# The two norms at the edge between mixer and feed-forward: fewer weight sums on TensorE, the head's steps in another order, and the last range written out by two queues

## The chip, the cores and the metric

The kernel runs on one core of a Trainium2 chip. The metric is the device time of one execution in microseconds (us). Before the change its median over three runs is 1840.19 us (1839.05 to 1841.2). About 0.2% of that, 3.7 us, is what a measurement of this kernel can tell from no change.

## What is computed

The reference is a two-layer encoder in fp32 that runs over a prompt of 256 positions and a sample of 512, both with 1024 channels. Layer 0 mixes positions with a bidirectional mLSTM, layer 1 with sliding-window attention. Behind each mixer stands a feed-forward block with a convolution of width 3 (2816 hidden channels), and at the end one more norm:

```
for l in range(2):
    h = rmsnorm(x, norm_g[l,0]) * (1+sc1) + sh1
    x = x + g1 * mixer_l(h)                        # ends with ... @ w_out
    h = rmsnorm(x, norm_g[l,1]) * (1+sc2) + sh2
    x = x + g2 * conv_ffn(h)                       # h @ w_up, conv, silu(g)*val, @ w_down
y = rmsnorm(x, final_g)
rmsnorm(x, g) = x * rsqrt(mean(x*x) + EPS) * g
```

The change touches the way in which the norm in front of each feed-forward block is made, the first steps of that block, and the last norm's output.

## The kernel before

**Layout.** Both sequences stand side by side in 768 columns; the 1024 channels are 8 chunks c of 128 partitions. Work on the columns goes in two HALVES of 384, or, at the end of the kernel, in RANGES of 256. A matrix product is made as three single-pass products of high and low parts (hi times hi, lo times hi, hi times lo). The high part of a tile is a ScalarE copy (L260) and the low part a VectorE subtraction (L261). TensorE (PE) issues in its program's order, and so does every other engine.

**The norm (class Norm, L90 to L165).** `square(c)` squares one chunk on ScalarE (L111 of the profile), and VectorE adds squares into one sum tile (L115) for as long as fewer than KC minus `on_pe` have come, so that `on_pe` squares stay apart. `stages()` sums over partitions with PE: for each of the three blocks of 128 columns one two-column matmul per remaining tile ("weight sums", `pa<-inv,nt`, 128x2). With `on_pe` = 2 three tiles remain, so nine matmuls, which the profile shows as 18 records. ScalarE then makes `nr` (L150), GpSimd (POOL) raises it to the power -1/2 (L153, "pow"), and three matmuls spread it over all partitions (`pa<-kct,nr`, "spread", six records). `apply` scales the half by the result.

**out_proj (L592 to L630)** makes 16 products of 128 channels: 0 to 7 for the first half, 8 to 15 for the second. Each is 24 matmuls into one of four PSUM banks in turn; behind it VectorE adds it to x (the residual, L590), and ScalarE squares the new chunk. The norm's remaining steps for the first half run between the second half's products (`tick`), with `combined`'s `apply` (L1095): 16 scalings L1090, a ScalarE bias, and a split into yh and yl. For the second half `apply` makes a longer chain (L1113, L1130, L1126 and so on), which begins with `dsh` (L1108), a subtraction of 4 numbers per partition.

**head (L1257 to L1369)** is the feed-forward block's start. It runs for PE, ScalarE and VectorE in the order in which it is written (`manual_schedule`). It takes `last_tile`, the rest of out_proj, which yields ahead of product 15. So what is in head ahead of `for _ in last_tile` (L1300) stands between product 14 and product 15 on PE: the two `mark` matmuls (`ps<-yh`, values that nothing reads) into banks 2 and 3, which held products 12 and 13. On VectorE stand there `sums(0)` (L1282 to L1287, sums of weights). Then come product 15, and `outset` (L1184), that is 12 products on the quarter B11 (the first half's chunks 0 to 3), a ScalarE copy of that bank (L1189), and 12 products on B21 into the same bank. Between B11 and B21 `step()` (L1306) puts the second half's nine weight sums, behind B21 its spread, and a second `outset` follows. `pair` (L1194) makes the following parts; its sums of weights are POOL's (L1202, L1205, L1206, L1214).

**The end.** The last RANGE's norm takes the spread factor `pr` in one PSUM bank. ScalarE copies it to SBUF (L574, `side`). POOL multiplies chunks 2, 5 and 7 by `side` (L579), VectorE the other five by `pr` (L581), and the sync engine (SP) issues the eight stores, in the order of c (L582).

## Time and profile before

| what | us |
|---|---|
| median of the three runs | 1840.19 |
| the profiled execution's own time | 1839.38 |
| its span, first to last instruction | 1837.3 |
| PE busy | 1792.4 (98%) |
| VectorE busy | 1373.0 (75%) |
| ScalarE busy | 893.9 (49%) |
| POOL busy | 486.6 (26%) |

Times within the execution are counted from the span's start. In rows of the timeline the first number is the start, the second the duration, and a bracket holds the idle time of the engine just before with what ended it. Rows of matmuls overlap, since one begins before the end of the other: the distance of starts is what one costs. Layer 0's head lies about 500 to 520, layer 1's about 1285 to 1305, and the end from 1828 on. The granted TensorE clock is 0.993 in the mean; in the last 12 us it is 0.50 to 0.63.

### The profile page before, as it was taken

How to read it: one execution, taken by the hardware profiler on the slowest of the kernel's cores; microseconds unless marked ns; L12 is line 12 of the kernel's file. 1: busy time of each engine (PE TensorE's matmuls, PEld its weight loads, DVE VectorE, ACT ScalarE, POOL GpSimd, SP SyncE). 2: the span in 40 equal slices, each digit the busy share in tenths (PEclk: the TensorE clock that was granted, in tenths of full speed). 3: DMA queues.
4: the chain of work that ended last, by engine and by line, in shares of the span. 5: the costliest groups of instructions: out<-in, count | busy, mean ns of one | idle time of the engine just before them, and what ended most of it. 6: DMA issues, size and time to landing. Idle time of an engine off the chain costs nothing.

```text
span 1837.3 us, 28927 instructions
## 1 busy us (share of the span) xinstructions
PE 1792.4 (98%) x11290; PEld 1657.9 (90%) x11290; DVE 1373.0 (75%) x2101; ACT 893.9 (49%) x1815; POOL 486.6 (26%) x386
## 2 busy tenths in 40 slices
PE   6999999999999999999999999999999999999997
PEld 3987887889998999999999999889889999999997
DVE  4755676886689877777777867766898777787876
ACT  4444443344456444444444557665464444444443
POOL 1001001031024333333331313320234333333322
PEclk9999999999999999999999999999999999999998
DMA  8344556546312212222222331234122222222212
GB/s 332 118 147 134 172 195 223 164 140 213 104 46 71 79 58 69 69 70 69 69 69 83 114 92 42 61 97 127 46 81 70 69 69 70 70 69 70 69 35 69
DMA packets 64245, 184.48 MB, mean 100 GB/s; under 512 B 6167, under 2 KB 23831, under 8 KB 64108
## 3 DMA queue, kind: packets, MB, share of 16 engines
q1 hardware_dynamic: 64108, 182.63, 30.7%
q8 instruction: 89, 1.46, 0.3%
q14 instruction: 48, 0.39, 0.1%
HBM read 176.17 MB, written 6.43 MB: 99 GB/s over the span
## 4 chain that ended last, share of the span: by engine, by line
PE 87%; DVE 5%; DMA 3%; ACT 2%; issue 1%; POOL 1%; SPq 0%; POOLq 0%; ACTq 0%; DVEq 0%
PE ps L254 29%; PE pa L254 24%; PE ps L1169 10%; PE ps L1172 10%; PE ps L1170 10%; PE pa L1008 1%; DMA slab<-in_adaln_w_dram 1%; DMA raw<-in_adaln_w_dram 1%; DMA raw<-in_w_dram 1%; DVE wlo L261 1%; DVE ada L506 1%; PE pa L1169 0%; PE pa L1172 0%; PE pa L1170 0%; DMA slab<-mrows 0%
## 5 line engine op out<-in xcount | busy, mean ns | idle before, releaser
L260 ACT CAST whi<-raw 128x1024 fp32r<-128x1024 f32 x237 | 247.9, 1048 | 344.2 <-PE pa L254 145.6
L261 DVE TENSOR_TENSOR wlo<-raw,whi 128x1024 fp32r<-128x1024 f32 x237 | 321.7, 1358 | 112.9 <-ACT whi L260 110.5
L254 PE MATMUL pa<-slab,whi 128*128 128x256 f32 (+1 forms) x1328 | 317.2, 334 | 0.0
L254 PEld LDWEIGHTS pa<-slab,whi 128*128 128x128 f32 x1328 | 230.2, 189 | 21.8 <-DVE slab L590 0.2
L590 DVE SCALAR_TENSOR_TENSOR slab<-pa,mod,slab 128x256 f32<-128x256 f32 (+1 forms) x332 | 192.8, 598 | 65.1 <-PE pa L254 65.0
L254 PE MATMUL pa<-slab,wlo 128*128 128x256 f32 (+1 forms) x664 | 212.7, 333 | 0.0
L254 PE MATMUL ps<-zh,whi 128*128 128x256 f32 (+1 forms) x560 | 189.2, 339 | 2.2 <-ACT whi L260 1.6
L254 PE MATMUL ps<-zh,wlo 128*128 128x256 f32 (+1 forms) x560 | 183.9, 330 | 1.7 <-DVE wlo L261 1.7
L254 PE MATMUL ps<-zl,whi 128*128 128x256 f32 (+1 forms) x560 | 185.0, 333 | 0.5 <-DVE zl L552 0.5
L1169 PE MATMUL ps<-zh,whi 128*128 128x384 f32 x504 | 172.2, 342 | 3.7 <-ACT nt L1240 1.9
L1170 PE MATMUL ps<-zl,whi 128*128 128x384 f32 x504 | 169.9, 337 | 1.8 <-DVE zl L1126 1.8
L1172 PE MATMUL ps<-zh,wlo 128*128 128x384 f32 x504 | 168.9, 335 | 0.0
L254 PE MATMUL ps<-slab,whi 128*128 128x384 f32 (+2 forms) x656 | 163.1, 332 | 0.9 <-DVE slab L261 0.5
L1205 POOL TENSOR_TENSOR raw<-raw,raw 128x512 f32<-128x512 f32 x40 | 52.0, 1299 | 331.0 <-DVE wlo L261 246.4
L254 PEld LDWEIGHTS pa<-slab,wlo 128*128 128x128 f32 x664 | 125.2, 189 | 12.6 <-DVE wlo L261 0.4
L1402 POOL TENSOR_TENSOR slab<-slab 128x772 f32<-128x772 f32 x44 | 86.5, 1968 | 166.0 <-DVE slab L1390 154.0
L1389 DVE SCALAR_TENSOR_TENSOR slab<-slab,cstt,slab 128x771 f32<-128x771 f32 x88 | 104.6, 1190 | 26.7 <-ACT slab L1387 26.5
L254 PEld LDWEIGHTS ps<-zh,whi 128*128 128x128 f32 x560 | 107.4, 192 | 15.8 <-issue 4.4
L506 DVE SCALAR_TENSOR_TENSOR ada<-raw,silc,ada 128x1024 f32<-128x1024 f32 x84 | 110.2, 1350 | 14.7 <-DMA raw<-in_adaln_w_dram 14.7
L254 PEld LDWEIGHTS ps<-zl,whi 128*128 128x128 f32 x560 | 107.4, 193 | 12.7 <-issue 3.4
L1202 POOL TENSOR_TENSOR raw<-raw 128x512 f32<-128x512 f32 x40 | 65.6, 1639 | 201.0 <-DMA raw<-in_w_dram 167.8
L254 PEld LDWEIGHTS ps<-slab,whi 128*128 128x128 f32 x656 | 115.1, 188 | 3.4 <-ACT whi L260 0.9
(291 smaller groups left out, 4336.7 us busy)
## 6 DMA issues: line engine op xcount, KB each, us to landing
raw<-in_w_dram SPq DMA_DIRECT2D x208, 512.0 KB, 3.7
raw<-in_adaln_w_dram SPq DMA_DIRECT2D x84, 512.0 KB, 4.6
slab<-in_x_dram SPq DMA_DIRECT2D x12, 512.0 KB, 7.9
slab<-in_adaln_w_dram SPq DMA_DIRECT2D x12, 512.0 KB, 10.2
slab<-mrows SPq DMA_DIRECT2D x8, 384.0 KB, 5.6
xs<-slab SPq DMA_DIRECT2D x6, 512.0 KB, 3.2
bt<-brow SPq DMA_DIRECT2D x16, 192.0 KB, 3.1
slab<-xs SPq DMA_DIRECT2D x6, 512.0 KB, 5.8
```

The source lines that it names most:

```text
L254: self.nc.tensor.matmul(out, lhsT, rhs, start=start, stop=stop)
L260: nc.scalar.copy(hi, src)
L261: return nc.vector.tensor_tensor(lo, src, hi.bitcast(F32), ALU.subtract)
L506: stt(acc[:, s], row, w, acc[:, s], ALU.mult, ALU.add)
L590: self.nc.vector.scalar_tensor_tensor(x, o, self.mod[l][:, gc + c, q : q + 1], x, ALU.mult, ALU.add)
L1169: mm(o, wh[:, k], hi[k], start=start and k == 0, stop=False, skip_group_check=True)
L1170: mm(o, wh[:, k], lo[k], start=False, stop=False, skip_group_check=True)
L1172: mm(o, wl[:, k], hi[k], start=False, stop=k == 3, skip_group_check=True)
L1202: tt(q[2], q[2], q[3], ALU.add)
L1205: tt(q[0], q[2], q[0], ALU.subtract)
L1389: stt(y[:, 1:], u[:, :-1], w(0), y[:, 1:], ALU.mult, ALU.add)
L1402: nc.gpsimd.tensor_tensor(y, y, yrow[:, j], ALU.mult)
```

## The change

1. `Norm` takes `on_pe` = 0 for the first half and 1 for the second: VectorE adds all eight squares, or seven, and three or six weight-sum matmuls remain. `held` keeps the add of the last two products out of `square`, so that head can place it; `begin` may put the first three of the second half's six ahead of B11.
2. `out_proj` yields ahead of product 14, and around the residuals of the last two products, and head uses that to place `sums(0)`, `sums(1)`, the splits, residuals and squares in an order of its own.
3. The `marks` therefore stand ahead of product 14 rather than ahead of 15.
4. The first `outset`'s quarters put their eight products with high weights first, then a step of the second half's norm (`low=step`), then the four with low weights.
5. `dsh` is made by the first half's `apply`.
6. POOL's pow is handed on as a third instruction to `behind`, so that `pair` for the first following part has its POOL work issued behind the second half's pow.
7. At the end the last range's factor is spread into two banks (`twin`); ScalarE copies the second, VectorE reads the first. Chunk 7 goes from POOL to VectorE; chunks 1, 2, 5 and 7 are stored by ScalarE's queue.

PE, the last two products in layer 0 (ps_4535 and ps_4536 are the banks of products 12 and 13, ps_4533 and ps_4534 those of 14 and 15). Before:

```order
L254 MATMUL ps_4533<-slab_3919,whi_5099 128x384 x2
L254 MATMUL ps_4533<-slab_3919,wlo_5100 128x384
L254 MATMUL ps_4535<-yh 128x384
L254 MATMUL ps_4536<-yh 128x384
L254 MATMUL ps_4534<-slab_3916,whi_5132 128x384 x2
L254 MATMUL ps_4534<-slab_3916,wlo_5133 128x384
```

and now:

```order
L266 MATMUL ps_4536<-slab_3919,whi_5063 128x384 x2
L266 MATMUL ps_4536<-slab_3919,wlo_5064 128x384
L266 MATMUL ps_4535<-yh 128x384
L266 MATMUL ps_4536<-yh 128x384
L266 MATMUL ps_4533<-slab_3916,whi_5097 128x384 x2
L266 MATMUL ps_4533<-slab_3916,wlo_5098 128x384
```

The marks have moved from behind product 14 to behind product 13, and the second mark now overwrites the bank that the matmul right ahead of it has just filled.

VectorE, around the residual of product 15 (ps_4534) and up to the second half's chain, before:

```order
L261 TENSOR_TENSOR wlo_5170<-raw_5145,whi_5169 128x1024
L590 TENSOR_SCALAR slab_4542<-ps_4534,mod_88,slab_4542 128x384
L1282 TENSOR_TENSOR raw_5151<-raw_5151 128x512
L1284 TENSOR_TENSOR raw_5149<-raw_5151,raw_5149 128x512
L1285 TENSOR_TENSOR raw_5149<-raw_5149 128x512
L1286 TENSOR_TENSOR slab_5142<-raw_5151,slab_5142 128x512
L1287 TENSOR_TENSOR raw_5151<-raw_5151,raw_5149 128x512
L261 TENSOR_TENSOR wlo_5233<-raw_5149,whi_5232 128x1024
L1108 TENSOR_TENSOR dsh<-mod_88 128x4
L1113 TENSOR_SCALAR slab_5254<-slab_4542,gain_91,pa_5250 128x384
```

and now:

```order
L1322 TENSOR_TENSOR wlo_5139<-raw_5116,whi_5138 128x1024
L120 TENSOR_TENSOR nt_4874<-nt_4874,nt_5166 128x384
L1308 TENSOR_TENSOR raw_5122<-raw_5122 128x512
L1310 TENSOR_TENSOR raw_5120<-raw_5122,raw_5120 128x512
L605 TENSOR_SCALAR slab_4542<-ps_4534,mod_88,slab_4542 128x384
L1312 TENSOR_TENSOR raw_5120<-raw_5120 128x512
L1314 TENSOR_TENSOR slab_5113<-raw_5122,slab_5113 128x512
L1315 TENSOR_TENSOR raw_5122<-raw_5122,raw_5120 128x512
L1322 TENSOR_TENSOR wlo_5208<-raw_5120,whi_5207 128x1024
L1139 TENSOR_SCALAR slab_5244<-slab_4542,gain_91,pa_5240 128x384
```

An add of squares (L120) and two of the sums have come ahead of the last residual, and the chain follows the last split at once, without `dsh`.

POOL at the same place, before (nr_5223 is the second half's factor; the raw tiles are weights of the following part):

```order
L153 TENSOR_TENSOR nr_4873<-nr_4873,mhalf 128x3
L1202 TENSOR_TENSOR raw_5579<-raw_5579 128x512
L1380 MEMSET slab_5136 128x4x4
L1380 MEMSET slab_5137 128x4x4
L1205 TENSOR_TENSOR raw_5581<-raw_5579,raw_5581 128x512
L153 TENSOR_TENSOR nr_5223<-nr_5223,mhalf 128x3
L1206 TENSOR_TENSOR raw_5581<-raw_5581 128x512
```

and now:

```order
L160 TENSOR_TENSOR nr_4870<-nr_4870,mhalf 128x3
L1420 MEMSET slab_5107 128x4x4
L1420 MEMSET slab_5108 128x4x4
L160 TENSOR_TENSOR nr_5224<-nr_5224,mhalf 128x3
L1228 TENSOR_TENSOR raw_5573<-raw_5573 128x512
L1231 TENSOR_TENSOR raw_5575<-raw_5573,raw_5575 128x512
L1232 TENSOR_TENSOR raw_5575<-raw_5575 128x512
```

The second half's power now stands ahead of the two sums of weights that it stood behind.

The diff, without its last hunk, which only hands `self.norm.power.ins` on as a third value of head:

```diff
@@ -110,10 +110,16 @@
         sq = net.tmp([P, self.n])
         net.nc.scalar.activation(sq, self.x(c), AF.Square)
         self.sums.append(sq)
-        if 2 <= len(self.sums) and self.count < KC - self.on_pe:
+        self.count += 1
+        if not self.held:
+            self.add()
+
+    def add(self):
+        if 2 <= len(self.sums) and self.count <= KC - self.on_pe:
             acc = self.sums[0]
             self.adds.tensor_tensor(acc, acc, self.sums.pop(), ALU.add)
-        self.count += 1
+
+    held = False
 
     count = 0
 
@@ -123,12 +129,13 @@
             self.pm = self.net.pa()
             self.sides = [self.pm[:, 2 * b : 2 * b + 2] for b in range(self.n // P)]
             self.done = 0
-        for i in range(self.done, n):
+        last = min(KC, self.on_pe + 1) - 1
+        for i in range(self.done, min(n, last + 1)):
             for b, o in enumerate(self.sides):
 
                 self.net.nc.tensor.matmul(
                     o, self.sums[i][:, b * P : (b + 1) * P], self.net.inv,
-                    start=i == b == 0, stop=i == KC - 1, skip_group_check=True,
+                    start=i == b == 0, stop=i == last, skip_group_check=True,
                 )
         self.done = max(self.done, n)
 
@@ -150,12 +157,17 @@
             nc.scalar.activation(r, mean, AF.Copy, bias=EPS)
         else:
             nc.vector.tensor_scalar(r, mean, EPS, None, ALU.add)
-        nc.gpsimd.tensor_tensor(r, r, net.mhalf[:, :nb], ALU.pow)
+        self.power = nc.gpsimd.tensor_tensor(r, r, net.mhalf[:, :nb], ALU.pow)
         yield 2.0
 
-        pr = net.pa()[:, : self.n]
-        for b in range(nb):
-            net.mm(pr[:, b * P : (b + 1) * P], r[:, b : b + 1].to_broadcast([P, P]), net.ident, True, True)
+        def spread():
+            pr = net.pa()[:, : self.n]
+            for b in range(nb):
+                net.mm(pr[:, b * P : (b + 1) * P], r[:, b : b + 1].to_broadcast([P, P]), net.ident, True, True)
+            return pr
+
+        pr = spread()
+        net.twin = spread() if self.on_pe == KC and self.last else None
         yield from self.apply(self.x, pr, self.rng)
 
     def run(self):
@@ -571,15 +583,18 @@
     def output(self, x, pr, rng):
         nc = self.nc
         side = self.tmp([P, rng[1] - rng[0]])
-        nc.scalar.copy(side, pr)
+        end = rng is RANGES[-1]
+        nc.scalar.copy(side, self.twin if end else pr)
         for c in range(KC):
 
-            if c in ((2, 5, 7), (0, 2))[rng is RANGES[1]]:
+            turn = c in ((2, 5, 7), (0, 2), (2, 5))[2 if end else rng is RANGES[1]]
+            if turn:
                 nc.scalar.activation(x(c), x(c), AF.Copy, scale=self.cst(FG + c))
                 nc.gpsimd.tensor_tensor(x(c), x(c), side, ALU.mult)
             else:
                 nc.vector.scalar_tensor_tensor(x(c), x(c), self.cst(FG + c), pr, ALU.mult, ALU.mult)
-            self.nc.sync.dma_start(self.io["y"][:, c, rng[0] : rng[1]], x(c))
+            queue = nc.scalar if end and c in (1, 2, 5, 7) else nc.sync
+            queue.dma_start(self.io["y"][:, c, rng[0] : rng[1]], x(c))
             if c % 2:
                 yield 1.3
 
@@ -606,7 +621,8 @@
                 for h, w in self.halves(u0 + u):
                     yield 1, 2 * u + h, w
 
-        norms = [Norm(self, xt, half, apply, last=True, adds=self.nc.vector) for half in HALVES]
+        norms = [Norm(self, xt, half, apply, i, last=True, adds=self.nc.vector) for i, half in enumerate(HALVES)]
+        self.norm = norms[1]
 
         self.turn = 1
         todo = tiles()
@@ -616,16 +632,26 @@
             for i, (z, c, w) in enumerate(first):
                 self.product(self.bank[2 + i][:, :H], w, act, 0, H, range(KC - 1))
                 self.begun[i] = KC - 1
-        for i, (z, c, w) in enumerate(todo):
-            if i in (KC, 2 * KC - 1):
+        soon = []
+        for i in range(2 * KC):
+            z, c, w = soon.pop() if soon else next(todo)
+            late = i >= 2 * KC - 2
+            if i == 2 * KC - 2:
+                soon.append(next(todo))
+            if i in (KC, 2 * KC - 2):
                 yield
             c0, c1, _ = HALVES[z]
             o = self.ps()[:, : c1 - c0]
             self.product(o, w, act, c0, c1, range(self.begun.pop(i, 0), KC))
             self.tick(4.2)
+            if late:
+                norms[z].held = True
+                yield
             for p0, p1, q in pieces(c0, c1):
                 self.resid(xt, o[:, p0 - c0 : p1 - c0], l, 16, c, (p0, p1, q))
             norms[z].square(c)
+            if late:
+                yield
             if i % KC == KC - 1:
                 self.start(HALVES[z], norms[z].stages())
 
@@ -1092,8 +1118,12 @@
                 )
                 nc.scalar.activation(b[:, s], b[:, s], AF.Identity, bias=sh)
 
+        dsh = pool.tile([P, 4], F32, name="dsh")
+
         def apply(x, pr, rng):
             if rng[0] == 0:
+                s = self.mod[l][:, 24 * i : 24 * i + 8, 0]
+                nc.vector.tensor_tensor(dsh, s[:, 4:], s[:, :4], ALU.subtract)
                 for c in range(KC):
                     full[c] = one(F32)
                     modulate(full[c], c, x, pr, rng)
@@ -1104,10 +1134,6 @@
             held = self.slab([P, KC, H])
             stt = nc.vector.scalar_tensor_tensor
             sh = lambda c: self.mod[l][:, 24 * i + c, q : q + 1]
-            dsh = pool.tile([P, 4], F32, name="dsh")
-            nc.vector.tensor_tensor(
-                dsh, self.mod[l][:, 24 * i + 4 : 24 * i + 8, q], self.mod[l][:, 24 * i : 24 * i + 4, q], ALU.subtract
-            )
 
             def scale(c):
                 stt(held[:, c], x(c), self.gain[l][i][:, c, q : q + 1], pr, ALU.mult, ALU.mult)
@@ -1181,14 +1207,14 @@
         for p0, p1, _ in pieces(0, H):
             self.nc.scalar.copy(r[:, col(p0) : col(p0) + p1 - p0], o[:, p0:p1])
 
-    def outset(self, o, w, r1):
+    def outset(self, o, w, r1, low=None):
 
 
         part = lambda i: [t[:, 512 * i : 512 * (i + 1)] for t in w]
-        self.quarters(o, part(0), self.B11, True)
+        self.quarters(o, part(0), self.B11, True, low)
         self.nc.scalar.copy(r1[:, col(H) :], o)
         yield
-        self.quarters(o, part(1), self.B21, False)
+        self.quarters(o, part(1), self.B21, False, low)
         self.evict(r1, o)
 
     def pair(self, pool, u, bank, rows, rest=False, behind=None):
@@ -1282,9 +1308,12 @@
             tt(s1_, s1_, a22, ALU.add)
             nc.scalar.copy(s1[i][0], s1_)
             tt(s2, s1_, s2, ALU.subtract)
+            yield
             tt(s4, s4, s2, ALU.subtract)
+            yield
             tt(s1[i][1], s1_, s1[i][0].bitcast(F32), ALU.subtract)
             tt(s1_, a22, s2, ALU.subtract)
+            yield
 
         def split(src, to=None):
 
@@ -1295,20 +1324,31 @@
         tt = nc.vector.tensor_tensor
         p5, u3 = ([self.tmp([P, H]) for _ in range(2)] for _ in range(2))
         wa[0] = self.split(ra[0])
-        sums(0)
-        wc[0] = self.split(ra[0])
+        ops = [sums(i) for i in range(2)]
+        next(ops[0])
+        next(ops[0])
+        wc[0], low = split(ra[0])
+        next(last_tile)
+        next(last_tile)
+        next(ops[0])
+        low()
+        self.norm.add()
+        next(last_tile)
+        self.norm.begin(1)
+        next(ops[1])
+        next(last_tile)
+        next(ops[1])
+        wc[1], low = split(ra[1])
+        next(ops[1])
+        low()
         for _ in last_tile:
             pass
         norm = self.take(HALVES[1])
         step = lambda n=1: [next(norm, None) for _ in range(n)]
-        first = self.outset(fixed(0), wa[0], rows[0][0])
+        first = self.outset(fixed(0), wa[0], rows[0][0], step)
         next(first)
-        step()
-        sums(1)
-        wc[1] = self.split(ra[1])
         next(first, None)
 
-        step()
         pa = lambda: self.pa()[:, :H]
         second = self.outset(pa(), wa[1], rows[1][0])
         next(second)
```

2 lines of the change are left out of this document (1 added, 1 removed).

## The prediction, made before the changed kernel ran

> **What bounds the kernel now.** I read the page's first part first: the busy time of each engine and its share of the span.
>
> ```profile
> PE 1792.4 (98%) x11290; PEld 1657.9 (90%) x11290; DVE 1373.0 (75%) x2101; ACT 893.9 (49%) x1815; POOL 486.6 (26%) x386
> ```
>
> PE is busy for 98% of the span, so a change pays if PE issues less, waits less, or the end behind its last matmul gets shorter. Next I read PE's waits around the two heads, the first two rows from 420 to 620 us (layer 0), the others from 1200 to 1400 us (layer 1). The columns are total, times, longest.
>
> ```profile
> PE ps L1170 <- DVE zl L1126: 0.4, 2, 0.2
> PE pa L254 <- POOL nr L153: 0.4, 1, 0.4
> ...
> PE ps L1170 <- DVE zl L1126: 1.4, 3, 1.0
> PE pa L254 <- POOL nr L153: 1.2, 1, 1.2
> ```
>
> The waits for `nr`, 0.4 and 1.2 us, are the ones at which the change aims. The wait for `zl` lies some 30 us behind the head, in the second half's chain.
>
> **Part 1: fewer weight sums, and what the marks take back.** From PE's timeline, layer 0: the first half's sums, the matmul behind them, and the second half's sums.
>
> ```profile
> 476.60 2.06 PE L254 MATMUL pa<-inv,nt 128*128 128x2 f32 x18
> 478.52 0.60 PE L254 MATMUL ps<-slab,whi 128*128 128x384 f32 x2
> ...
> 511.17 2.06 PE L254 MATMUL pa<-inv,nt 128*128 128x2 f32 x18
> ```
>
> Eighteen records take 478.52 - 476.60 = 1.92 us, so six take 0.64 and twelve 1.28. The first half goes from 18 to 6: 1.28 us less on PE, per layer. The VectorE adds that replace them (0.55 us each in its timeline, below) fall ahead of the scalings, where VectorE waits for others.
>
> But the marks move to a place behind product 13, and the second mark writes the bank that product 13 has just filled. It must wait for that product's residual. The rows are the last record of product 13, the marks (both PE), then VectorE from ahead of the scalings on.
>
> ```profile
> 500.15 0.34 PE L254 MATMUL ps<-slab,wlo 128*128 128x384 f32 x1
> ...
> 504.54 0.51 PE L254 MATMUL ps<-yh 128*128 128x384 f32 x2
> ```
>
> ```profile
> 483.96 1.23 DVE L261 TENSOR_TENSOR wlo<-raw,whi 128x1024 fp32r<-128x1024 f32 x1 [0.33 <-ACT whi L260]
> ...
> 500.53 0.62 DVE L590 SCALAR_TENSOR_TENSOR slab<-ps,mod,slab 128x384 f32<-128x384 f32 x1
> 501.06 0.55 DVE L115 TENSOR_TENSOR nt<-nt,nt 128x384 f32<-128x384 f32 x1
> ```
>
> Before, the residual of product 13 ran at 500.53 and the marks came 4 us later, so they never waited. Now product 13's last record starts at 500.15 - 1.28 = 498.87. Records follow each other by 0.17, so the first mark stands at 499.04 and the second could go at 499.21. The residual starts at 500.53 - 1.28 = 499.25 at best, ends at 499.87, and PE resumes about 0.06 later (the pow and the spread of part 2 show that step: 514.47 + 1.31 = 515.78, then 515.84), at 499.93. That is a wait of 0.72 us. The first record behind a stall takes 0.42 rather than 0.34, 0.08 more. So 1.28 - 0.80 = 0.48 us stay. VectorE's timeline has no idle time from 483.96 to past 501, so it may also be the later one: ScalarE's splits do not all move with it, and I allow it 0.4 us, which leaves 0.08. I take the middle: **0.3 us a layer**, from 0.1 to 0.5. Every microsecond by which VectorE is later costs PE one.
>
> **Part 2: the second half's sums, pow and spread.** PE's rows are the start of B11, the spread, and the start of the second outset; the last is layer 1's spread. Behind them ScalarE's last square and its copy of B11, POOL's rows (the first is the first half's pow) and VectorE's.
>
> ```profile
> 509.08 0.34 PE L1169 MATMUL ps<-yh,whi 128*128 128x384 f32 x1
> ...
> 515.84 0.94 PE L254 MATMUL pa<-kct,nr 128*128 128x128 f32 x6 [0.41 <-POOL nr L153]
> 516.53 0.42 PE L1169 MATMUL pa<-yh,zh 128*128 128x384 f32 x1
> ...
> 1301.35 0.93 PE L254 MATMUL pa<-kct,nr 128*128 128x128 f32 x6 [1.16 <-POOL nr L153]
> ```
>
> ```profile
> 509.98 0.53 ACT L111 ACTIVATE nt<-slab 128x384 f32<-128x384 f32 x1 [1.86 <-DVE slab L590]
> 511.37 0.48 ACT L1189 COPY slab<-ps 128x384 f32<-128x384 f32 x1 [0.86 <-PE ps L1172]
> ```
>
> ```profile
> 478.95 0.85 POOL L153 TENSOR_TENSOR nr<-nr,mhalf 128x3 f32<-128x3 f32 x1 [37.87 <-ACT nr L150]
> ...
> 513.23 1.28 POOL L1205 TENSOR_TENSOR raw<-raw,raw 128x512 f32<-128x512 f32 x1 [5.89 <-DMA raw<-in_w_dram]
> 514.47 1.31 POOL L153 TENSOR_TENSOR nr<-nr,mhalf 128x3 f32<-128x3 f32 x1
> 515.76 2.31 POOL L1206 TENSOR_TENSOR raw<-raw 128x512 f32<-128x512 f32 x1
> ```
>
> ```profile
> 505.27 0.95 DVE L1284 TENSOR_TENSOR raw<-raw,raw 128x512 f32<-128x512 f32 x1
> ...
> 509.33 0.61 DVE L590 SCALAR_TENSOR_TENSOR slab<-ps,mod,slab 128x384 f32<-128x384 f32 x1
> ...
> 516.84 1.25 DVE L1108 TENSOR_TENSOR dsh<-mod 128x4 f32<-128x4 f32 x1
> ```
>
> Before, from the start of B11 to the second outset: 516.53 - 509.08 = 7.45 us in layer 0. In layer 1 the wait for pow is 0.75 longer (1.16 against 0.41): 8.20. Now, with PE at B11 at t:
>
> - Three sums ahead, 0.64. Eight products, 8 x 0.173 (twelve take 2.09, 511.17 - 509.08) = 1.39. The other three sums, 0.64. Four products, 0.70. B11's bank is complete at t + 3.37.
> - ScalarE's copy of this bank must end before B21 may write it. Before, it ran from 511.37 to 511.85 under the sums and cost nothing. Now nothing stands between: it starts 0.20 behind the slot that follows B11's last record (511.37 against 511.17, where the sums stand), the copy takes 0.48, the restart 0.06 and 0.08. That is 0.82 us of **new wait**. B21 begins at t + 4.19.
> - Eight products (1.39), spread (516.53 - 515.84 = 0.69), four products (0.70): the second outset at t + 6.97.
>
> Does the pow come in time? The sums end at t + 2.67; before, the pow stood behind L1205, which had waited for a transfer, and ran for 1.31 beside VectorE; the first half's quiet pow began 478.95 - 478.52 = 0.43 behind its sums and took 0.85. So the factor is there at t + 3.95, or t + 4.41 with the slower 1.31; PE wants it at t + 5.58. The wait for POOL goes, in both layers, and what is late next is the copy above. Gain of part 2: 7.45 - 6.97 = **0.5 us in layer 0**, 8.20 - 6.97 = **1.2 in layer 1**.
>
> Do VectorE and ScalarE deliver? Before, four sums of weights and a split stood between the residuals of products 14 and 15, from 505.27 to 509.33: 4.06. Now it is again four sums and a split, and an add of 0.55: at most 4.6, say 4.5. With PE 0.3 earlier they begin at 505.0, so the last residual starts near 509.5 rather than 509.0. It takes 0.61 and its square 0.53: done at 510.6; PE wants it at t + 2.03 = 510.8. The add, which the first three sums read, stands two sums of weights ahead (some 1.4), near 508.1; PE wants it at 508.8. The slack is 0.2; what VectorE is late beyond that PE waits in full, queued behind the second sums with the low products and B21.
>
> **Part 3: dsh and the chain.** The chain behind the spread would start some 2.8 us earlier: 1.25 from `dsh`, the rest from the sums and splits now placed ahead. I price it at nothing: the chain is the same in both layers, and yet PE waits 0.4 for its `zl` in one and 1.4 in the other, 1.0 of it in one piece. So these waits are not set by the chain's start, and an earlier start does not take them away. At its new place `dsh` is a 4-element subtraction ahead of the first residual; from 0 to 1.25, and I take 0, since VectorE idles a quarter of the span.
>
> What `dsh` cost is weighed here. It lasts 1.25 us for 4 elements, 516.84 to 518.09, and POOL's L1206 beside it ends at 515.76 + 2.31 = 518.07. The Trainium skill, "SBUF — State Buffer", section "SBUF: two separate sides", says that VectorE and GpSimd share a port pair as an exclusive lock, which a VectorE operation with two SBUF inputs takes only against a GpSimd operation that reads SBUF, and that the loser blocks for the whole instruction; the trace agrees, with 518.09 against 518.07. By that rule dsh's price is a remainder of POOL's, which passes to the chain's next such operation, and removing dsh saves nothing by itself; the sum would be the same.
>
> **Part 4: the end.** PE's spread, ScalarE's copy, VectorE's and POOL's products, and SP's issues.
>
> ```profile
> 1829.09 1.22 PE L254 MATMUL pa<-kct,nr 128*128 128x128 f32 x4 [1.04 <-POOL nr L153]
> 1830.35 0.37 ACT L574 COPY nt<-pa 128x256 f32<-128x256 f32 x1 [2.09 <-PE pa L254]
> 1830.76 2.05 DVE L581 SCALAR_TENSOR_TENSOR slab<-slab,cstt,pa 128x256 f32<-128x256 f32 x5 [5.07 <-ACT nt L574]
> 1830.80 2.09 POOL L579 TENSOR_TENSOR slab<-slab,nt 128x256 f32<-128x256 f32 x3 [1.76 <-ACT nt L574]
> ```
>
> ```profile
> 1831.26 3.79 SPq L582 DMA_DIRECT2D out_dram<-slab  x8
> ```
>
> SP issues eight stores in 3.79 us, about 0.48 each, done at 1835.05; the span ends 2.25 later, at 1837.3. All products are done by 1832.9, so the issuing sets the end. Now VectorE starts at 1830.35 without waiting for ScalarE and does six products of 0.41: done at 1832.8. The second spread ends some 0.95 behind the first, ScalarE's copy at 1831.7, POOL's two products of 0.70 at 1833.1. SP has four stores and is done by 1833.0. ScalarE's queue issues chunks 1, 2, 5, 7: chunk 5 at 1833.15, chunk 7 behind it, done at about 1834.1 if an issue there costs what it does on SP. With the same 2.25: 1836.3, **1.0 us** earlier. ScalarE's own price of an issue isn't in the trace; at half of SP's, 0.24, chunk 7 is issued by 1833.6, and at double, 0.96, four issues from 1831.7 end at 1835.5, so the gain is between 1.4 and -0.5.
>
> **The sum.** 2 x 0.3 + 0.5 + 1.2 + 1.0 = 3.3 us less. The execution profiled took 1839.38 in its own time (span 1837.3 and 2.1 around it), so 1836.1 for one like it; it lies 0.8 under the median, and from the median the time is 1840.19 - 3.3 = **1836.9 us**, 0.18% less.
>
> **The rivals.**
>
> - *The marks cost nothing* (the second mark's wait is for less than I think): the first half keeps 1.28 in both layers, 1.9 more in all, so 1835.0. Against it: the residual cannot start before product 13 ends, by data. For it: only the wait of the second mark is derived from order, not seen.
> - *The tail gives nothing*, because an issue on ScalarE costs 0.84, 1.75 times SP's (1831.7 + 4 x 0.84 = 1835.05): 1837.9. For it: the first store on ScalarE waits for the copy, 0.9 later than SP's first one may go. Against it: ScalarE does nothing else there.
> - *The chain collides elsewhere*: layer 0 waited 0.4 for `zl` and layer 1 waited 1.4, 1.0 of it in one piece. POOL's work of the next part now starts at another time, so each layer may get or lose that 1.0: from 1835.9 (layer 1 loses it) to 1837.9 (layer 0 gets it).
> - *Slower: VectorE is late at the mark.* Place: the residual of product 13, which PE now waits for 4 us sooner than before. If the first half's scalings don't start 1.28 earlier (they wait for ScalarE's part), and `dsh` and two of the adds fall into VectorE's gapless stretch (1.25 and 2 x 0.5), it is 1.28 + 2.2 = 3.5 us late, and PE loses 7.0 over both layers against gains of 2 x 0.48 + 1.7 + 1.0 = 3.7: 3.3 slower than before, 1843.5. It decides at 3.7 / 2 = 1.85 us late per layer. Against it: the gap of 0.33 at 483.96, ahead of which dsh and the adds stand, and the page's 75%.
>
> **How the numbers follow.** Forecast 0.60, the marks' rival 0.14, the tail's 0.12, the chain's 0.07, slower 0.07. The range of the forecast's unknowns (part 1 by 0.4 in all, part 4 from -0.5 to 1.4, the chain by 1.0 either way) is 1835.1 to 1839.8; the runs before lie up to 1.1 off their median, so I give **1834.0 to 1840.0**, which takes in the first three rivals. A measurement of this kernel can tell about 0.2%, 3.7 us, from no change; that is 1836.5, close under the forecast: about two fifths of the forecast's case (0.23) and the marks' rival lie below it, and of the slower one's 0.07 some 0.04 lie above 1843.9, so faster 0.38, within 0.2% 0.58, slower 0.04.
>
> **What would show it.** Right: the marks' row of PE with about 0.7 to 1.1 us of wait for VectorE's residual in each layer; six records where eighteen stood; no wait for `nr` in the second half; about 0.7 of wait for ScalarE ahead of B21; the second outset some 0.8 us earlier in layer 0 and 1.5 in layer 1 against the same point; the last store issued near 1834. Wrong: no wait at the marks, or one of over 1.85 us; a wait for squares at the second sums; a longer wait for `zl`; or stores that still end 2.25 us behind 1835.

## The result, and the profile after

The changed kernel takes 1835.05 us in the median of 12 runs (1833.05 to 1840.33), the kernel before 1839.26 (1836.36 to 1841.2, 12 runs). The ratio is 0.998 with a 95% interval of 0.9971 to 0.9989, so the change saves some 3.7 us, between 2.0 and 5.3. The forecast was 3.3, or 1836.9 us counted from the median of the first three runs.

The profiled execution of the changed kernel is its slowest, 1840.33, with a span of 1838.5 us against 1837.3 before. Its excess lies ahead of everything that the change touches. The rows are the same point of layer 0 in front of out_proj, first before, then after (PE's timeline):

```profile
435.43 0.60 PE L523 MATMUL ps<-kct,sb 128*128 128x128 f32 x4
```

```profile
440.25 0.60 PE L535 MATMUL ps<-kct,sb 128*128 128x128 f32 x4
```

It is 4.8 us behind there. TensorE had a lower granted clock on the way. The windows view shows one such stretch (the columns are the length, the busy time of PE, PEld, DVE, ACT and POOL with counts, then PEclk, DMA share, GB/s); before, then after:

```profile
35.00:45.00 10.00, 9.56 (x53) 8.97 (x53) 9.56 (x30) 9.29 (x26) 0.00 (x0) 0.73 0.61 242
```

```profile
35.00:45.00 10.00, 9.56 (x47) 8.93 (x48) 9.18 (x29) 9.66 (x27) 0.00 (x0) 0.66 0.69 272
```

These ten microseconds alone make 0.7 us (0.07 of 10). Over the whole way to that point, the trace's record of the clock has 10.2 us at half speed before and 20.5 after. Half of the difference is 5.1 us, which accounts for the 4.8. So spans of two executions say little here; what follows compares distances between points inside one trace.

PE's waits of the changed kernel, 420 to 620 us and then 1200 to 1400:

```profile
PE ps L266 <- DVE slab L605: 0.9, 1, 0.9
...
PE ps L1195 <- ACT slab L1215: 0.6, 1, 0.6
PE ps L1196 <- DVE zl L1152: 0.4, 2, 0.2
```

```profile
PE ps L1196 <- DVE zl L1152: 1.4, 3, 1.0
PE ps L266 <- DVE slab L605: 1.0, 1, 1.0
...
PE ps L1195 <- ACT slab L1215: 0.6, 1, 0.6
```

The waits for `nr` are gone. In their place are the two new ones that the forecast named, for the residual at the marks (L605) and for ScalarE's copy of B11's bank (L1215). The waits for `zl` are what they were. Here is PE's timeline through layer 0's head:

```profile
482.83 0.72 PE L266 MATMUL pa<-inv,nt 128*128 128x2 f32 x6
483.41 0.42 PE L266 MATMUL ps<-slab,wlo 128*128 128x384 f32 x1
...
503.62 0.33 PE L266 MATMUL ps<-slab,wlo 128*128 128x384 f32 x1
503.79 0.34 PE L266 MATMUL ps<-yh 128*128 128x384 f32 x1
505.04 0.44 PE L266 MATMUL ps<-yh 128*128 128x384 f32 x1 [0.91 <-DVE slab L605]
...
513.72 0.72 PE L136 MATMUL pa<-inv,nt 128*128 128x2 f32 x6
514.31 0.42 PE L1195 MATMUL ps<-yh,whi 128*128 128x384 f32 x1
...
515.79 0.77 PE L136 MATMUL pa<-inv,nt 128*128 128x2 f32 x6
...
517.93 0.44 PE L1195 MATMUL ps<-yh,whi 128*128 128x384 f32 x1 [0.57 <-ACT slab L1215]
...
519.44 0.83 PE L266 MATMUL pa<-kct,nr 128*128 128x128 f32 x6
...
520.81 0.34 PE L1195 MATMUL pa<-yh,zh 128*128 128x384 f32 x1
```

VectorE's residual of product 13, for which the second mark waits, and POOL's pow:

```profile
504.37 0.61 DVE L605 SCALAR_TENSOR_TENSOR slab<-ps,mod,slab 128x384 f32<-128x384 f32 x1
```

```profile
517.07 1.82 POOL L160 TENSOR_TENSOR nr<-nr,mhalf 128x3 f32<-128x3 f32 x1 [5.12 <-ACT nr L157]
```

Six records where eighteen stood, 0.58 us; then the second mark stands 1.25 us behind the first, where 0.17 would do; then the split sums, the copy, the spread without a bracket, and the second outset at 520.81. Counted from the point in front of out_proj, product 13's last record is 1.35 us earlier than before (503.62 - 440.25 against 500.15 - 435.43), B11's part of the head starts 0.18 earlier (513.72 against 509.08), and the second outset 0.54 (520.81 against 516.53). In layer 1 the same distance to the second outset is 1.15 shorter. The experiments below count to the second product of that outset instead, which takes in that the first one, right behind the spread, was slower before (0.25 us to the next, now 0.17): 0.63 and 1.22.

The end, all engines:

```profile
1831.49 2.07 PE L266 MATMUL pa<-kct,nr 128*128 128x128 f32 x8 [1.03 <-POOL nr L160]
1832.75 2.44 DVE L595 SCALAR_TENSOR_TENSOR slab<-slab,cstt,pa 128x256 f32<-128x256 f32 x6 [4.67 <-PE pa L266]
1833.60 0.37 ACT L587 COPY nt<-pa 128x256 f32<-128x256 f32 x1 [2.94 <-PE pa L266]
1833.66 2.67 ACTq L597 DMA_DIRECT2D out_dram<-slab  x4
1834.05 1.40 POOL L593 TENSOR_TENSOR slab<-slab,nt 128x256 f32<-128x256 f32 x2 [2.61 <-ACT nt L587]
```

VectorE starts behind PE, no longer behind ScalarE. The last store is issued by ScalarE at 1833.66 + 2.67 = 1836.33, 4.84 behind the spread's start, and the span ends 2.2 later. Before it was 1835.05, 5.96 behind, and 2.2. From the spread to the end it is 7.1 us instead of 8.2. What sets the end now is POOL's second product, which ends at 1834.05 + 1.40 = 1835.45: ScalarE issues the store of that chunk and the last one behind it.

These terms make 0.54 + 1.15 + 1.1 = 2.8 us. But there is a fourth that no step of the forecast contains. Between the heads the PE program is the same, yet its points drift: the second outset of layer 0 is 4.28 behind that of the execution before (520.81 against 516.53), and the start of layer 1's out_proj only 3.1. Another 1.2 us go the same way between layer 1's head and the end, with the same waits. Over two stretches well clear of the heads, from about 550 to 1200 and from 1380 to 1800 us, it is 1.05 and 1.22. The next view has TensorE's products on the tile `bq`, with minimum, median and maximum duration in ns (a product overlaps the next; the distances from start to start, below, differ by as much). Before:

```profile
L1169 PE MATMUL ps<-bq,whi x168: 332/338/444, 537.9 to 1779.9; 128*128 128x384 f32 x168
L1169 PE MATMUL ps<-zh,s1h x160: 336/338/342, 527.0 to 1771.4; 128*128 128x384 f32 x160
```

and after:

```profile
L1195 PE MATMUL ps<-bq,whi x168: 331/335/439, 542.1 to 1780.5; 128*128 128x384 f32 x168
L1195 PE MATMUL ps<-zh,s1h x160: 331/336/340, 531.2 to 1772.1; 128*128 128x384 f32 x160
```

The products that read `bq`, `s1h` or `s1l`, some 1030 in the feed-forward parts of both layers, are shorter. From start to start, in gapless rows, they went from means of 175.7 to 176.7 ns, by group, to 173.4 to 174.3. The groups' differences times their counts make 2.6 us, which is about what the two stretches show (2.3). Four experiments below look for the reason.

### The profile page after: what moved, and what is told of

Read it like the earlier page. It is cut to its first block, busy times and chain, and to the rows that moved or that the text cites. A ratio compares the mean times of both kernels' runs of the same rounds, so it can differ in the third digit from the quotient of the medians.

```text
span 1838.5 us, 28868 instructions
## 1 busy us (share of the span) xinstructions
PE 1793.5 (98%) x11258; PEld 1657.8 (90%) x11258; DVE 1376.2 (75%) x2108; ACT 893.2 (49%) x1814; POOL 484.5 (26%) x385
## 4 chain that ended last, share of the span: by engine, by line
PE 84%; DVE 6%; issue 4%; ACT 3%; DMA 2%; POOL 1%; SPq 0%; POOLq 0%; DVEq 0%; ACTq 0%
PE ps L266 26%; PE pa L266 24%; PE ps L1195 10%; PE ps L1196 10%; PE ps L1198 10%; PE pa L1034 1%; DMA slab<-in_adaln_w_dram 1%; DVE wlo L273 1%; DMA raw<-in_adaln_w_dram 1%; ACT bq L1119 1%; ACT whi L272 1%; DVE ada L518 1%; PE pa L1198 0%; PE pa L1196 0%; PE pa L1195 0%
## 5 line engine op out<-in xcount | busy, mean ns | idle before, releaser
L272 ACT CAST whi<-raw 128x1024 fp32r<-128x1024 f32 x233 | 243.8, 1049 | 334.6 <-PE pa L266 145.3
L273 DVE TENSOR_TENSOR wlo<-raw,whi 128x1024 fp32r<-128x1024 f32 x233 | 315.5, 1355 | 109.5 <-ACT whi L272 107.5
L605 DVE SCALAR_TENSOR_TENSOR slab<-pa,mod,slab 128x256 f32<-128x256 f32 (+1 forms) x332 | 192.7, 598 | 65.1 <-PE pa L266 64.9
L1429 DVE SCALAR_TENSOR_TENSOR slab<-slab,cstt,slab 128x771 f32<-128x771 f32 x88 | 108.7, 1237 | 26.7 <-ACT slab L1427 26.4
L266 PEld LDWEIGHTS ps<-zh,wlo 128*128 128x128 f32 x560 | 107.8, 193 | 12.9 <-DVE wlo L273 3.6
## 6 DMA issues: line engine op xcount, KB each, us to landing
slab<-in_adaln_w_dram SPq DMA_DIRECT2D x12, 512.0 KB, 10.2
```

The costliest lines, as they stand in the source:

```text
L266: self.nc.tensor.matmul(out, lhsT, rhs, start=start, stop=stop)
L272: nc.scalar.copy(hi, src)
L273: return nc.vector.tensor_tensor(lo, src, hi.bitcast(F32), ALU.subtract)
L605: self.nc.vector.scalar_tensor_tensor(x, o, self.mod[l][:, gc + c, q : q + 1], x, ALU.mult, ALU.add)
L1429: stt(y[:, 1:], u[:, :-1], w(0), y[:, 1:], ALU.mult, ALU.add)
```

## The experiments

The theory at this point: each part does what the forecast says, and the two new waits on PE are paid in full, so that the same sums in another order would give more. The rivals: that PE's time in the heads isn't what counts (something else is late then), that the end's gain is chance, and, for the drift, that it has to do with the head's order or is chance. All ratios are to the kernel before.

**The marks behind product 14 again.** The edit, in the changed kernel:

```diff
-        for t in banks[0][1:]:
-            mark(t)
 ...
         next(last_tile)
         next(last_tile)
+        for t in banks[0][1:]:
+            mark(t)
```

> The changed kernel with the marks put back behind product 14, and nothing else. Theory (the marks' wait for the residual of product 13 is paid on TensorE in full, 0.91 us and 1.01 us in the changed kernel's trace, plus a restart): no wait at the marks, the last two products about 1.1 us earlier in each layer, 2.2 us less than the changed kernel, so about 6 us below the kernel before, ratio 0.9967. Rival (VectorE, which is the later one there, delays product 15's bank or the last residual instead, and the wait only moves): a wait for VectorE appears ahead of product 14 or 15 or at the second sums, and the time is that of the changed kernel, ratio 0.998.

Measured: 0.9969 (0.9957 to 0.9981), median 1834.62. No wait at the marks is left in either layer; the copy's waits stand at 0.6. Against the same point in front of out_proj, layer 0's second outset is 1.45 us earlier than in the kernel before, instead of 0.63, and layer 1's 2.06 instead of 1.22. So the mark's wait was worth 0.8 us a layer, not 1.1. Part of it comes back: PE's second sums start 0.43 and 0.36 us behind the product ahead of them, where 0.17 would do, since PE now catches up with the last residual and its square. These gaps are too short for the waits' view. The wait for `zl` in layer 1 was 0.4 instead of 1.4 in this execution. The theory holds in the place; by the runs alone, 0.9969 and 0.998, the two kernels' intervals overlap.

**All six sums between B11 and B21.**

```diff
-        self.norm.begin(1)
 ...
-        first = self.outset(fixed(0), wa[0], rows[0][0], step)
+        first = self.outset(fixed(0), wa[0], rows[0][0])
         next(first)
+        step()
         next(first, None)
+        step()
```

> The changed kernel with the first outset in its old order: all twelve products on B11, then the six weight sums at one place, then the twelve products on B21, then the spread. Theory (ScalarE's copy of B11's bank, which the changed kernel waits for, 0.6 us by the trace and 0.8 with the restart, is hidden beneath 1.28 us of sums, and the pow, in time 5.5 us behind, is not waited for since POOL has nothing ahead of it): 0.8 us less in each layer than the changed kernel, ratio to the kernel before about 0.9971. Rival (the low products were needed to cover the pow, 1.82 us in the changed kernel): a wait for nr of 0.5 us or more returns, and little is gained, ratio 0.998.

Measured: 0.9958 (0.9945 to 0.9972), median 1832.09. PE's rows in layer 0 are the sums, B21, and the spread:

```profile
512.30 1.39 PE L266 MATMUL pa<-inv,nt 128*128 128x2 f32 x12
...
513.84 0.45 PE L1195 MATMUL ps<-yh,whi 128*128 128x384 f32 x1
...
516.04 0.83 PE L266 MATMUL pa<-kct,nr 128*128 128x128 f32 x6
```

No bracket at B21: the sums cover the copy, but for about 0.1 us (B21 starts 1.54 behind the sums, and 1.42 in the last run of this section). None at the spread: the pow is in time without the low products in between. By the traces each layer is 0.57 us shorter than in the changed kernel (1.20 and 1.79 against 0.63 and 1.22). So the split order of part 4 of the change costs more than it brings. The runs show more than the traces, 4 us against 1.1, and their interval only just reaches that; I take the trace for the size.

**The end alone**, put into the kernel before (the hunks of `stages` and `output`).

> The kernel before with the end's part of the change alone: the second spread, chunk 7 on VectorE, four stores issued by ScalarE. Theory (issues set the end; the span ends 7.0 us behind the last spread instead of 8.2): 1.2 us less than the kernel before, ratio 0.9993. Rival (what the end gains is lost to the second spread at half clock, or the gain in the profile is chance): no difference, ratio 1.000.

Measured: 0.9995 (0.9986 to 1.0004), median 1839.48 against 1840.62. The runs don't separate 1.1 us from nothing. In the trace the pow's end and the span's end are 7.11 us apart, as in the changed kernel, and 8.23 in the kernel before. So the end gives 1.1 us where it can be seen by itself.

**The head alone**: the changed kernel with the old `output` and no `twin`.

> The changed kernel with the end as it was. Theory (0.5 us in layer 0 and 1.2 us in layer 1 by the two traces): 1.7 us less than the kernel before, ratio 0.9991, and end and head add up to the whole change. Rival (the head gives more than the two traces show, since the changed kernel's median lies some 4 us under): 2.5 to 3 us less, ratio 0.9985.

Measured: 0.9982 (0.9973 to 0.999), median 1837.11, 3.3 us less: the rival's size. The trace shows the same heads (0.63 and 1.28 us) and again the drift, 1.04 and 1.21 us over the two stretches where the trace of the whole change has 1.05 and 1.22. The trace of the end alone has 0.10 and 0.10. So the drift comes with what the kernels with the new head have in common.

**Both edits**, the marks and the sums.

> The changed kernel with both edits of the first two runs: the marks behind product 14, and all six weight sums between B11 and B21. Theory (two separate waits on TensorE, 1.1 us and 0.7 us in each layer, that add up): 3.6 us less than the changed kernel, ratio to the kernel before 0.9960; by the two runs' own ratios, if they add up, 0.9947. Rival (with TensorE 1.8 us earlier, VectorE's last residual or the pow becomes the bound): a wait for nr or for squares returns, and the ratio stays at 0.9965 or above.

Measured: 0.9957 (0.9943 to 0.9971), median 1831.85, no better than the sums alone by the runs. In the trace the heads are 2.03 and 2.61 us shorter than before. That is 0.8 more than with the sums alone, not the 1.1 of the theory, and the reason is seen in ScalarE's rows:

```profile
512.19 0.53 ACT L111 ACTIVATE nt<-slab 128x384 f32<-128x384 f32 x1 [0.59 <-DVE slab L605]
512.92 1.04 ACT L1319 CAST whi<-raw 128x1024 fp32r<-128x1024 f32 x1 [0.20 <-DVE raw L1310]
513.88 0.47 ACT L1215 COPY slab<-ps 128x384 f32<-128x384 f32 x1
```

The copy that PE waits for is queued behind a split's copy of 1.04 us that nobody waits for yet, and B21 waits 0.35. So the rival has a part in it: another engine did become the bound, ScalarE by its order.

**The place of dsh, in the kernel before.** The change creates the tile `dsh` ahead of `bq`, `s1h` and `s1l` in their pool. Its 16 bytes take a slot of 32, so these ten tiles (`bq` is eight) move from byte 212928 (a multiple of 64) and so on to 32 above. This edit moves the tile in the kernel before and leaves the operation where it was:

```diff
+        dsh = pool.tile([P, 4], F32, name="dsh")
+
         def apply(x, pr, rng):
             if rng[0] == 0:
 ...
-            dsh = pool.tile([P, 4], F32, name="dsh")
             nc.vector.tensor_tensor(
```

> The kernel before in which the 16 bytes of the tile dsh are allocated ahead of the feed-forward tiles bq, s1h and s1l, as the changed kernel does, and not behind them; the operation itself stays where it was, and every engine's order is that of the kernel before. The tiles move by 32 bytes, from multiples of 64 to 32 above one. Theory (by the traces the products that read bq or s1h take 176 ns each in the kernel before and in the kernel with the end's part alone, 173.5 in all kernels with the new head, over some 800 products): 2.3 us less than the kernel before, ratio 0.9988, with 173.5 ns in those rows. Rival (the pace is set by the new head's order, or differs by chance between executions): 176 ns as before, ratio 1.000.

Measured: 0.9986 (0.9977 to 0.9996), median 1837.41: 2.6 us less, with every engine's order unchanged. The products' view, for `bq` and for `s1h`:

```profile
L1170 PE MATMUL ps<-bq,whi x168: 331/335/440, 538.1 to 1776.1; 128*128 128x384 f32 x168
L1170 PE MATMUL ps<-zh,s1h x160: 331/336/340, 527.3 to 1767.7; 128*128 128x384 f32 x160
```

The durations are those of the changed kernel, and so is the drift (1.06 and 1.23 us). This settles where the drift comes from: a line of the diff that reads as bookkeeping is worth 2.3 us by the traces, more than the end or either head. Of the 2.6 us by the runs not all need be the place's, since in this execution PE also waited 0.4 less for `nr` in each layer and 1.0 less for `zl` in layer 1.

**bq back, in the changed kernel**: `dsh` is created behind `bq`, so that `bq` stands on multiples of 64 again and `s1h` does not.

```diff
+                full[0] = one(F32)
+                box.append(pool.tile([P, 4], F32, name="dsh"))
-                nc.vector.tensor_tensor(dsh, s[:, 4:], s[:, :4], ALU.subtract)
+                nc.vector.tensor_tensor(box[0], s[:, 4:], s[:, :4], ALU.subtract)
```

> The changed kernel with dsh allocated behind bq, so that the eight bq tiles stand on multiples of 64 bytes again, while s1h and s1l stay 32 above; every engine's order is that of the changed kernel. Theory (the place of a tile sets the pace of the products that read it): products on bq at 176.5 ns, products on s1h at 173.5 to 174.5, 1.1 us more than the changed kernel, ratio to the kernel before 0.9986. Rival (place has nothing to do with it): both rows at 173.5, ratio 0.998.

Measured: 0.9982 (0.9972 to 0.9992); the runs don't tell the two expectations apart. The view does:

```profile
L1197 PE MATMUL ps<-bq,whi x168: 335/338/444, 539.3 to 1778.2; 128*128 128x384 f32 x168
L1197 PE MATMUL ps<-zh,s1h x160: 331/336/340, 528.4 to 1769.8; 128*128 128x384 f32 x160
```

`bq` is slow again, `s1h` stays quick, and of the drift 0.36 and 0.37 us are left instead of 1.05 and 1.22. (The wait for `zl` in layer 1 was 1.0 shorter here, which hides this in the runs.)

**yh and yl moved too**: the kernel with both edits, `dsh` created ahead of these two.

```diff
+            self.dsh = pool.tile([P, 4], F32, name="dsh")
             self.yh = pool.tile([P, 2, 4, H], R, name="yh")
```

> The kernel with both edits, with dsh allocated ahead of yh and yl too, so that these, which stand on multiples of 64 bytes in all kernels so far, move by 32; every engine's order is that of the kernel with both edits. Theory (the same 2.5 ns on each of the some 850 products that read yh or yl): 2 us less than the kernel with both edits, ratio to the kernel before 0.9948 by the sum of the traces or 0.9936 by the runs' ratios. Rival (the pace of the yh products has another cause, since they are the first of a bank): no difference to the kernel with both edits.

Measured: 0.996 (0.9945 to 0.9974), the same as with both edits. The products on `yh` went from a median of 338 to 335:

```profile
L1193 PE MATMUL ps<-yh,whi x304: 331/335/522, 508.7 to 1769.2; 128*128 128x384 f32 x152
```

and the two stretches are shorter by 0.54 and 0.51 us more than with both edits, half of the 2 us expected. From start to start only `yh` with `whi` gained the full 2.3 ns (175.4 to 173.1); `yl` with `whi` gained 1.1 and `yh` with `wlo` 0.4, and the products of `yh` and `yl` with `zh` and `zl` gained nothing (173.2 to 173.7 with both edits, 174.8 to 174.9 here). In this execution PE also had half its clock for 3.4 us in layer 1's head (the maximum of 522 is from there), which took the gain back in the trace. The runs don't show a gain of 1 us.

**Everything moved by 32 bytes**: `inv` and `mhalf` of the changed kernel in one tile, so that all later tiles start 32 lower.

```diff
-        self.inv = cp.tile([P, 2], F32, name="inv")
+        both = cp.tile([P, 8], F32, name="inv")
+        self.inv, self.mhalf = both[:, :2], both[:, 2:]
 ...
-        self.mhalf = cp.tile([P, 8], F32, name="mhalf")
```

> The changed kernel with inv and mhalf in one tile, so that every later tile in SBUF moves by 32 bytes: zh, zl, whi, wlo, bq, s1h and s1l come to stand on multiples of 64, yh and yl 32 above; every engine's order but for VectorE's two first fills is that of the changed kernel. Theory A (a tile on a multiple of 64 bytes makes the products that read it slower, whatever the other operand): most products at 176 ns and more, some 7000 of them, 15 to 20 us more than the changed kernel, ratio to the kernel before about 1.007. Theory B (the moving and the stationary operand must stand alike to each other): products on zh, bq and s1h with whi at 173 to 174.5 as in the changed kernel, those on yh at 176, ratio 0.998.

Measured: 0.9976 (0.9967 to 0.9986), median 1835.27: theory A, 15 us and more, falls. With `bq`, `s1h`, `zh` and the weights all on multiples of 64 the products are as quick as with all of them 32 above:

```profile
L1195 PE MATMUL ps<-bq,whi x168: 331/335/440, 537.0 to 1774.3; 128*128 128x384 f32 x168
L1195 PE MATMUL ps<-yh,whi x304: 332/338/440, 509.2 to 1770.2; 128*128 128x384 f32 x152
```

`yh`, which stands 32 above now (`yl` too), is the slow one. So the absolute place doesn't count. For the products that read `bq`, `s1h`, `s1l` or, with `whi`, `yh` and `yl`, it is whether the two operands stand alike to 64 bytes, as theory B says. A general rule it is not: `yh` and `yl` with `zh` or `zl` are as quick 32 bytes off (173.1 to 174.4 ns here and before). Why the place matters at all, no run shows.

**POOL's order undone**: the changed kernel without `self.norm.power.ins` in what head hands on.

> The changed kernel without the pow as a third instruction that POOL's following work waits for: L1228 and L1231 stand ahead of the pow again. Theory (the pow is 0.5 us ahead of the spread in the changed kernel, and L1231 holds POOL for 1.3 from a transfer's landing on): a wait of TensorE for nr returns, up to 0.8 us in a layer, 0 to 1.6 us in all. Rival (TensorE reaches the spread late enough anyhow, because of the copy): no wait for nr in either layer, so that POOL's order gave nothing.

Measured in a single execution: 1840.79 us. PE's waits, layer 0 and layer 1, and POOL's rows:

```profile
PE pa L266 <- POOL nr L160: 1.7, 1, 1.7
```

```profile
514.91 1.54 POOL L1231 TENSOR_TENSOR raw<-raw,raw 128x512 f32<-128x512 f32 x1 [4.67 <-DMA raw<-in_w_dram]
516.53 2.13 POOL L1232 TENSOR_TENSOR raw<-raw 128x512 f32<-128x512 f32 x1
518.63 0.86 POOL L160 TENSOR_TENSOR nr<-nr,mhalf 128x3 f32<-128x3 f32 x1
```

Layer 1 has the same 1.7. The wait is twice what I expected, because L1232 goes ahead of the pow as well. The heads are 1.9 us longer than in the changed kernel (1.28 longer than before the change in layer 0, 0.67 in layer 1). So this order is no trimming: without it, in this trace, the new head loses.

**Fewer sums alone**, in the kernel before: `on_pe` of 0 and 1 and the new `begin`, nothing else by hand.

```diff
-        norms = [Norm(self, xt, half, apply, last=True, adds=self.nc.vector) for half in HALVES]
+        norms = [Norm(self, xt, half, apply, i, last=True, adds=self.nc.vector) for i, half in enumerate(HALVES)]
```

> The kernel before with three weight sums for the first half and six for the second, and no other part of the change: the marks stay behind product 14, the order of the head is the old one. Theory (the first half's 1.28 us are kept in both layers where the marks don't wait; of the second half's 0.64 nothing is kept, since the wait for the pow, which stands behind L1205, grows by as much): 2.6 us less than the kernel before, ratio 0.9986, waits for nr of 1.0 and 1.8 us. Rival (VectorE, which has the added squares' sums, becomes late at the last residual): waits for VectorE at products 14 or 15, ratio 1.000.

Measured: 0.9983 (0.9974 to 0.9992), median 1836.41. The expected size, but not as I had it: the waits for `nr` don't grow, they go. The pow now runs ahead of L1206 (then L1205):

```profile
513.97 0.86 POOL L154 TENSOR_TENSOR nr<-nr,mhalf 128x3 f32<-128x3 f32 x1 [5.68 <-ACT nr L151]
515.09 1.28 POOL L1206 TENSOR_TENSOR raw<-raw,raw 128x512 f32<-128x512 f32 x1 [0.26 <-DMA raw<-in_w_dram]
```

POOL's order isn't written by hand, and in the program that this edit makes the pow stands ahead of L1206. So this run has two things at once, fewer sums and the pow's new place, and no run has the first without the second.

At the second outset PE is 2.55 us ahead of the kernel before in layer 0 and 3.11 in layer 1. Some 5 us on it gives 0.95 of it back, waiting 0.7 for a bank's copy (L1190) that stands on ScalarE behind the first `zh`, which the late chain brings late. That wait is not there in the last run below, which has PE as far ahead (2.53 and 3.15) and the earlier chain; which part of the change takes it away was not tested by itself. (`dsh` took only 0.15 us in layer 0 of this execution.) The net is 1.6 and 2.1 us, more than the whole of the new head's 0.6 and 1.2.

**The best of all**: both edits, `yh` and `yl` moved, and the last split behind the copy of B11's bank.

```diff
-        wc[1], low = split(ra[1])
         next(ops[1])
-        low()
 ...
         next(first)
         step()
+        wc[1] = self.split(ra[1])
         next(first, None)
```

> The kernel with both edits and with yh and yl moved by 32 bytes, in which the split of the second weight for B22 (a 1.04 us copy on ScalarE and a subtraction on VectorE) comes behind the copy of B11's bank and the second sums rather than ahead. Theory (in the kernel with both edits that copy runs 0.5 us late, queued on ScalarE behind the split's, and TensorE waits 0.35 us at B21): no wait there, 0.4 us a layer less than that kernel, and 1.1 us less by the moved tiles; with everything, 6 to 8 us less than the kernel before, ratio 0.9960 to 0.9945. Rival (the chain, which begins behind the split on VectorE, comes later and its wait for zl grows): no gain over the kernel with both edits, 0.9957.

Measured: 0.9946 (0.9933 to 0.996), median 1828.92 (1828.62 to 1831.79): 9.9 us below the kernel before, by fewer sums, the order of the work, the end and the place of tiles. By the trace its heads are 2.53 and 3.15 us shorter than before (2.03 and 2.61 with both edits), no wait stands at the marks, at B21 or at the spread, and `zl` waits 0.4 in both layers.

## Why the prediction was right, point by point

- *Fewer sums, 1.28 us a layer*: right. 18 records became 6, and product 13 ended 1.35 earlier.
- *The marks take most of it back, 0.3 left*: right in place, a little low in size. The waits are 0.91 and 1.01 us, forecast from 0.72 to 1.12. VectorE's residual began 0.75 behind the start of product 13's last record (504.37 - 503.62), against 0.38 before; that is the lateness of 0.4 that was allowed. With the restart 0.18 was left in layer 0 and nothing in layer 1, which is below the 0.1 to 0.5 forecast. That this wait is paid on PE is shown by the run with the marks moved back, though it gives only 0.8 of it.
- *The copy, a new wait of 0.8*: right. The bracket says 0.57, and from B11's part to the second outset it took 7.09 us where 6.97 were forecast. That the sums covered the copy before is shown by the run with the sums between.
- *No wait for the pow*: right, and the slack was smaller than I had it. The pow took 1.82 us, not 0.85 to 1.31, beside VectorE's split, which ended 0.71 before it, and was ready 0.55 ahead of the spread. That it needs POOL's order is shown by the run that undoes it.
- *VectorE in time for the last square*: right, by 0.12 us. The square ended at 515.67, and PE's second sums began at 515.79.
- *dsh at nothing*: **this is the step that failed.** For the operation it was right: at its new place it took 0.15 us, and the earlier chain left the waits for `zl` at 0.4 and 1.4. As the Trainium skill has it ("SBUF — State Buffer", section "SBUF: two separate sides"), the loser of the port pair blocks for the other's whole instruction; by that rule dsh's 1.25 us pass to the next VectorE operations with two SBUF inputs. The trace agrees: the chain's first two L1156 and its first L1152 took 0.96, 1.01 and 1.65 us beside POOL, 0.62, 0.62 and 0.55 otherwise, 1.83 us more. So does the run with fewer sums alone: `dsh`, still at its old place there, took 0.15, and two VectorE operations ahead of it 1.76 and 2.31 beside POOL instead of 0.69 and 1.22. But the forecast priced only the operation. The line that creates the tile moved ten other tiles by 32 bytes, and that took 2.3 us from PE in the feed-forward parts, which the sum had as untouched. The run with the place alone gave 2.6 (0.7 to 4.2).
- *The end, 1.0*: 1.1 by the traces. ScalarE's four issues, with their waits, took 2.67 us, and the span ended 2.2 behind the last.
- *The sum*: 0.6 + 1.7 + 1.0 were forecast. The traces have 0.2 for part 1, 1.5 for part 2, 1.1 for the end, and 2.3 that weren't in it: 5.1. The runs have 3.7, from 2.0 to 5.3. That the total came so near to the forecast is partly luck: its own terms make 2.8 rather than 3.3, a term of 2.3 is missing, and the runs' interval holds both 2.8 and 5.1. No run has the whole new head with all ten tiles at their old places.
- *The rivals*: VectorE was not late beyond a microsecond, the end gave its microsecond, and `zl` stayed at 0.4 and 1.4; but in eight of the experiments it was 0.4 in both layers. The traces show what the 1.0 us is. In layer 1 of the kernel before:

```profile
1329.88 2.32 DVE L1126 TENSOR_TENSOR zl<-slab,zh 128x384 fp32r<-128x384 f32 x2
```

```profile
1330.51 1.28 POOL L1205 TENSOR_TENSOR raw<-raw,raw 128x512 f32<-128x512 f32 x1 [22.93 <-ACT zh L1120]
```

The second of the two `zl` starts at 1330.54, 0.03 behind POOL's sum of weights, and takes 1.66 us instead of 0.56. In all six traces with 1.4 POOL's sum starts 0.03 to 0.06 us ahead of that `zl`; in all eight with 0.4 it starts from 0.01 ahead to 0.3 behind, and the `zl` takes 0.56. So a margin of some 0.05 us decides 1.0, and the change did not decide it. The single traces of two kernels may differ by this 1.0 for that reason alone.

What stays open: the runs with the sums between are some 3 us better than the trace explains, at the edge of the interval. The race for `zl` may hold 1.0 of that, but only one execution of each kernel was traced.

## What to carry to other kernels

Where an engine is 98% busy, try each part of a change alone: fewer sums alone gave 1.6 and 2.1 us in the heads, the whole new head 0.6 and 1.2. Read a moved wait as a cost at its new place: here the sums saved on TensorE were worth 1.3 us a layer, and a wait of 1.0 came with a marker that moved by one product. Look at ScalarE's queue ahead of the instruction that TensorE waits for; a split that nobody needs yet can stand in front of it. And when a diff creates a tile earlier, compare the places of all tiles behind it, and the median duration of the matmuls that read them, before giving any change of time to the order of work.

## What the runs showed of the hardware

Products of 128x384 that read `bq`, `s1h` or `s1l` followed each other by 173.4 to 174.3 ns (means by pair of operands, from start to start in gapless rows) when moving and stationary operand stood alike to 64 bytes, both on a multiple or both 32 above, and by 175.6 to 176.7 when one stood 32 off the other. `yh` with `whi` went from 175.4 to 176.0 down to 173.1. Products of `yh` or `yl` with `zh` or `zl` don't follow this: 173.1 to 174.4 unlike, 174.0 to 174.9 alike.

A VectorE subtraction of two SBUF tiles took 0.56 us when it started level with or ahead of a sum on POOL, and 1.62 to 1.66 when that sum had started 0.03 to 0.06 us before it.

Pieces of 3.4 us, or two or three in a row, at half the granted clock cost 1.7 us each. Their number differs between executions: three ahead of layer 0's out_proj in the kernel before, six in the changed kernel. They made the changed kernel's profiled span longer than the one before though its median is 4 us lower.
